# The expert stage of a streaming-encoder layer: weight splits in pieces of 1024 columns instead of 512, products with the high part of a weight first

## The chip, the cores and the metric

The program runs on one core of one Trainium2 chip. Its time is the device time of one execution in microseconds (us); the kernel before was executed three times for it. One further execution was recorded by the hardware profiler, and all rows below are from that record. The engines are named as in the profile: PE multiplies matrices (PEld is its weight load), ACT and DVE are the scalar and the vector engine, POOL and SP issue transfers here, each in the order in which its instructions stand.

## The reference

One layer of an encoder over 1024 tokens of 1024 features in float32: a mixer (pooling branch and gated recurrent branch), then a mixture of experts, then a norm. The change lies in the mixture. Each token is routed to two of 32 experts, and each expert computes, for its tokens:

```python
xt = rmsnorm(x, g_ffn).reshape(T, D)               # T = 1024, D = 1024
# top-1 group of 4, then the top-2 experts of its 8 -> expert_id, gate
hid = silu(xb @ w_gate[e]) * (xb @ w_up[e])        # (128, 1024) @ (1024, 512), twice
yb  = hid @ w_down[e]                              # (128, 512) @ (512, 1024)
y   = zeros((T, D)).at[tok].add(yb * gate)         # weighted sum of a token's two experts
```

Each expert has 6 MiB of float32 weights: 2 MiB each of gate, up and down.

## The kernel before

The program has two parts. The mixer and the router run first, on two halves of 512 tokens; their instructions are the same before and after the change. The expert stage follows, from about 713 us to 1303 us of the span, and a final norm ends the program.

**The stage.** A block of 128 token slots is computed for every expert (a dynamic loop ahead of the stage would take further blocks, L1245; it ran no iteration in this record). For expert e, PE's order is written out by hand (L1341 to 1365): `gate_up(e, 0)`, in whose middle `htrans(e - 1)` transposes the hidden values of the expert before; `gate_up(e, 1)`; `xtrans(e + 1)`, which transposes the next expert's tokens; and `down(e - 1)`. The order on ACT and DVE is made by a scheduler when the program is built. SP's and POOL's order around the stage is that of the code.

**Products in three parts.** PE gets a float32 matrix as a high part, rounded to the format fp32r, and a low part that holds the rest. `split` (L224) makes them: ACT copies the source into the high part (L225), DVE subtracts the high part from the source (L226). `mm3` (L243) multiplies high by high (L244), high by low (L245) and low by high (L246), 512 columns each, into one PSUM tile. One expert has 48 such products for gate and up (tiles `gu`) and 24 for down (tiles `y`), 72 in all.

**Pieces.** `piece` (L1172) splits one 512-column quarter of a weight slot: tiles `whi` (high) and `wlo` (low) of 512 columns, four buffers each. An expert takes 24 pieces. A piece's buffers are free once its three products are done. The tokens are split in `xtrans` (L1161), four transposes and one split of 512 columns at a time, in two PSUM tiles of tag `tr`; the hidden values in `htrans` (L1201), a third user of `tr`. `down` (L1213) has two PSUM tiles of 512 columns (tag `yo`), which ACT copies out by two instructions (L1224) before POOL scatters the rows to `yd` (L1228).

**Weight slots.** Weights come in transfers of 1 MiB, six for an expert, in the order in which they are used. `RING` (L932) lists 18 slots: 17 in memory that the mixer leaves, the last, `rawm`, in the stage's own. SP issues the transfer for the slot 18 further on when the slot's last piece has been split (L1177). Slots 0 to 16 are filled while the mixer ends, slot 17 (`load(17)`, L1237) just ahead of the stage.

**Entry and end.** Four pieces are split ahead of the first product, two before the dynamic loop (L1242) and two behind it (L1329). The first expert has no `down` in front of it, so expert 1's tokens are needed right after their transposes. At the end, `htrans(31)` and `down(31)` follow `down(30)` directly.

Of the kernel before, what the change touches and what calls it, by code (L numbers as in the profile page):

```python
# [10 lines left out]
F32 = mybir.dt.float32  # L11
F32R = mybir.dt.float32r
# [3 lines left out]
AF = mybir.ActivationFunctionType  # L16
# [24 lines left out]
def kernel(  # L41
# [4 lines left out]
    nc = tc.nc  # L46
# [17 lines left out]
    identf = cp.tile([P, P], F32, name="identf")  # L64
# [15 lines left out]
    rp = ctx.enter_context(tc.tile_pool(name="rp", bufs=2, side="right"))  # L80
    b8 = ctx.enter_context(tc.tile_pool(name="b8", bufs=4, side="right"))
# [161 lines left out]
    def mm3(o, ah, al, bh, bl, first, last):  # L243
        nc.tensor.matmul(o, ah, bh, start=first, stop=False)  # L244
        nc.tensor.matmul(o, ah, bl, start=False, stop=False)  # L245
        nc.tensor.matmul(o, al, bh, start=False, stop=last)  # L246
# [682 lines left out]
        eng.tensor_tensor(gates[:, hg, 0:1], q[0], q[1], op=OP.add)  # L929
        eng.tensor_tensor(gates[:, hg, 1:2], q[2], gates[:, hg, 0:1], op=OP.subtract)  # L930

    RING = (("t4", 2, 0), ("b2", 1, 0), ("r0", 3, 1), ("b2", 1, 0), ("r1", 6, 1), ("b8", 4, 2), ("rawm", 1, 3))  # L932
    ring = [(tag, pool) for tag, n, pool in RING for _ in range(n)]
    RA = len(ring)
    raws = {}
# [7 lines left out]

    def rawslot(n, shape, name):
        tag, pool = ring[n % RA]
        pool = rp if pool == 0 else b8 if pool == 2 else mp if pool == 3 else r0 if tag == "r0" else r1
        return pool.tile(shape, F32, name=name, tag=tag, bufs=2 if pool is rp else dict((a, b) for a, b, _ in RING)[tag])

    def load(n, q=nc.sync):
# [184 lines left out]
    for tag, shape, dt, bufs in (("xy", [D], F32, 4), ("xl", [2, FE], F32, 1), ("xh", [KT, P], F32, 1), ("hp", [2, 2, P], F32, 1),  # L1134
                                 ("hh", [4, P], F32, 1), ("hl", [4, P], F32, 1), ("whi", [FE], F32R, 4),
                                 ("rawm", [4, FE], F32, 1), ("wlo", [FE], F32R, 4)):
        ts = [mp.tile([P] + shape, dt, name=f"{tag}_{n}", tag=tag, bufs=bufs) for n in range(bufs)]
        if tag == "xy":
            xy = ts
        elif tag == "rawm":  # L1140
            raws[17] = ts[0]
        elif tag in ("wlo", "whi"):
            early[tag] = ts
        else:
            ov[tag] = ts[0]
# [15 lines left out]
    def xtrans(e):  # L1161
        xg = xgs[e]
        xh = mt([P, KT, P], F32R, f"xh{e}", "xh", 1)
        xl = mt([P, KT, P], F32R, f"xl{e}", "xl", 1)
        for k2 in range(2):
            tp = mq.tile([P, 4, P], F32, name=f"tp{e}{k2}", tag="tr", bufs=2)
            for k in range(4):
                nc.tensor.transpose(tp[:, k, :], xg[:, (4 * k2 + k) * P:(4 * k2 + k + 1) * P], identf)  # L1168
            split(xh[:, 4 * k2:4 * k2 + 4, :], xl[:, 4 * k2:4 * k2 + 4, :], tp)
        st["x", e] = (xh, xl)  # L1170

    def piece(ec, k, ld=True):  # L1172
        if (ec, k) in pre:
            return pre.pop((ec, k))
        n = where[ec]
        if ld and k == 0 and n + RA < 6 * NE:
            load(n + RA)  # L1177
        hi = mt([P, FE], F32R, f"wh{n}{k}", "whi", 4)
        lo = mt([P, FE], F32R, f"wl{n}{k}", "wlo", 4)
        split(hi, lo, raws[n][:, k, :])  # L1180
        return hi, lo

    def gate_up(e, n, mid=None):
        xh, xl = st["x", e]
        o = mq.tile([P, FE], F32, name=f"gu{e}{n}", tag="gu", bufs=4)
        for c in range(2):
            for k in range(4):
                wh, wl = piece((e, 2 * n + c), k)
                kk = 4 * c + k
                mm3(o, xh[:, kk, :], xl[:, kk, :], wh, wl, kk == 0, kk == KT - 1)  # L1190
                if mid and kk == 3:
                    mid[0](*mid[1:])
# [7 lines left out]

    def htrans(e):  # L1201
        hp = st["hp", e]
        tp = mq.tile([P, 4, P], F32, name=f"th{e}", tag="tr", bufs=2)
        for k in range(4):
            nc.tensor.transpose(tp[:, k, :], hp[:, k // 2, k % 2, :], identf)
        hh = mt([P, 4, P], F32R, f"hh{e}", "hh", 1)
        hl = mt([P, 4, P], F32R, f"hl{e}", "hl", 1)
        split(hh, hl, tp)
        st["h", e] = (hh, hl)
# [2 lines left out]

    def down(e):  # L1213
        hh, hl = st["h", e]
        yo = [mq.tile([P, 512], F32, name=f"y{e}{n}", tag="yo", bufs=2) for n in range(2)]
        for c in range(2):
            for k in range(2):
                kk = 2 * c + k
                for n in range(2):
                    wh, wl = piece((e, 4 + c), 2 * k + n)  # L1220
                    mm3(yo[n], hh[:, kk, :], hl[:, kk, :], wh, wl, kk == 0, kk == 3)
        ys = next_xy()
        for n in range(2):
            nc.scalar.activation(ys[:, n * 512:(n + 1) * 512], yo[n], AF.Copy)  # L1224
        return ys

    def scatter(e, ys):
# [17 lines left out]
    with tc.For_i(0, nov, 1) as it:  # L1245
# [15 lines left out]
        oidp = mq.tile([P, 2, 1], F32, name="oidp", tag="tr", bufs=2)  # L1261
# [11 lines left out]
        xg = xy[2]  # L1273
# [5 lines left out]
        for k2 in range(2):  # L1279
            tp = mq.tile([P, 4, P], F32, name="otp", tag="tr", bufs=2)  # L1280
            for k in range(4):
                nc.tensor.transpose(tp[:, k, :], xg[:, (4 * k2 + k) * P:(4 * k2 + k + 1) * P], identf)
            nc.vector.tensor_copy(xT[:, 4 * k2:4 * k2 + 4, :], tp)
# [19 lines left out]
        tp = mq.tile([P, 4, P], F32, name="otp", tag="tr", bufs=2)  # L1303
# [159 lines left out]
```

## Time and profile before

| | |
|---|---|
| time, median of 3 runs | 1349.5 us (1348.29 to 1351.13) |
| profiled execution, first to last instruction | 1349.2 us (the record gives no other time of it) |
| PE busy over the span | 1270.6 us, 94% |
| DVE busy over the span | 1023.3 us, 76% |
| ACT busy over the span | 828.6 us, 61% |
| last chain, share by engine | PE 88%, DVE 6%, DMA 3% |
| expert stage, 740 to 1290 us: PE / DVE / ACT busy | 549.9 / 519.2 / 519.8 of 550 us |
| granted PE clock in that stretch | 1.00 |

How to read it: the shares over the span mix a mixer, in which ACT and DVE have room, with a stage in which three engines are busy nearly all the time. Products on PE overlap, so the duration of one (about 0.39 us) says less than the distance from its start to the next one's start. "Idle" in a row is the time in which an engine had nothing to do ahead of the row's instruction, and the arrow names what ended it.

### The profile page before, as it was taken

How to read it: one execution, taken by the hardware profiler on the slowest of the kernel's cores; microseconds unless marked ns; L12 is line 12 of the kernel's file. 1: busy time of each engine (PE TensorE's matmuls, PEld its weight loads, DVE VectorE, ACT ScalarE, POOL GpSimd, SP SyncE). 2: the span in 40 equal slices, each digit the busy share in tenths (PEclk: the TensorE clock that was granted, in tenths of full speed). 3: DMA queues.
4: the chain of work that ended last, by engine and by line, in shares of the span. 5: the costliest groups of instructions: out<-in, count | busy, mean ns of one | idle time of the engine just before them, and what ended most of it. 6: DMA issues, size and time to landing. Idle time of an engine off the chain costs nothing.

```text
span 1349.2 us, 18579 instructions
## 1 busy us (share of the span) xinstructions
PE 1270.6 (94%) x6342; PEld 1050.6 (78%) x6342; DVE 1023.3 (76%) x1917; ACT 828.6 (61%) x1381; POOL 136.4 (10%) x209
## 2 busy tenths in 40 slices
PE   7999999999999999999968999999999999999960
PEld 6879888888988988888756777878777787877740
DVE  4586873456598687344287999999999999999977
ACT  5433422343533242233257999999999999999964
POOL 3110000000011000000042011011011101011004
PEclk9999999999999999999978999999999999999985
DMA  7332223344453222544767999999999999999255
GB/s 221 77 101 79 63 76 89 105 158 154 133 194 94 79 63 79 187 125 147 305 220 265 352 379 373 374 372 364 367 369 367 383 376 374 384 377 378 84 192 230
DMA packets 130698, 307.16 MB, mean 228 GB/s; under 512 B 15229, under 2 KB 89513, under 8 KB 106026
## 3 DMA queue, kind: packets, MB, share of 16 engines
q1 hardware_dynamic: 120378, 281.82, 59.0%
q0 software_dynamic: 9216, 16.80, 3.4%
q10 hardware_dynamic: 1008, 7.34, 1.4%
q8 instruction: 50, 0.82, 0.2%
q14 instruction: 46, 0.38, 0.1%
HBM read 295.43 MB, written 27.26 MB: 239 GB/s over the span
## 4 chain that ended last, share of the span: by engine, by line
PE 88%; DVE 6%; DMA 3%; ACT 1%; issue 1%; POOL 0%; SPq 0%; ACTq 0%; DVEq 0%; POOLq 0%
PE gu L245 9%; PE gu L246 9%; PE gu L244 8%; PE y L245 5%; PE y L246 4%; PE y L244 4%; PE ga L244 2%; PE ga L246 2%; PE ga L245 2%; PE gb L245 2%; PE gb L244 2%; PE gb L246 2%; PE vo L244 2%; PE tp L1168 2%; PE vo L245 2%; PE vo L246 2%
## 5 line engine op out<-in xcount | busy, mean ns | idle before, releaser
L226 DVE TENSOR_TENSOR wl<-rw,wh 128x512 fp32r<-128x512 f32 x760 | 477.0, 685 | 34.7 <-ACT wh L225 34.6
L225 ACT ACTIVATE wh<-rw 128x512 fp32r<-128x512 f32 x760 | 463.0, 631 | 32.6 <-PE y L246 11.9
L245 PE MATMUL gu<-wl,xh 128*128 128x512 f32 x508 | 201.6, 397 | 0.2 <-DVE wl L226 0.2
L244 PE MATMUL gu<-wh,xh 128*128 128x512 f32 x508 | 201.0, 396 | 0.8 <-ACT wh L225 0.4
L246 PE MATMUL gu<-wh,xl 128*128 128x512 f32 x508 | 198.7, 391 | 0.0
L245 PEld LDWEIGHTS gu<-wl,xh 128*128 128x128 f32 x508 | 95.4, 188 | 32.3 <-DVE wl L226 12.8
L244 PEld LDWEIGHTS gu<-wh,xh 128*128 128x128 f32 x508 | 95.4, 188 | 20.4 <-ACT wh L225 0.9
L246 PEld LDWEIGHTS gu<-wh,xl 128*128 128x128 f32 x508 | 95.4, 188 | 18.2 <-DVE xl L226 0.5
L244 PE MATMUL y<-wh,hh 128*128 128x512 f32 x256 | 102.7, 401 | 1.1 <-ACT hh L225 1.1
L245 PE MATMUL y<-wl,hh 128*128 128x512 f32 x256 | 103.5, 404 | 0.1
L246 PE MATMUL y<-wh,hl 128*128 128x512 f32 x256 | 100.6, 393 | 0.0
L245 PEld LDWEIGHTS y<-wl,hh 128*128 128x128 f32 x256 | 48.1, 188 | 21.6 <-DVE wl L226 12.4
L1157 POOL DMA_INDIRECT xy<-xtd,src x32 | 32.8, 1024 | 295.2 <-PE tp L1168 294.1
L244 PEld LDWEIGHTS y<-wh,hh 128*128 128x128 f32 x256 | 48.1, 188 | 10.7 <-ACT hh L225 1.3
L1228 POOL DMA_INDIRECT yd<-xy,dst x32 | 32.2, 1005 | 230.1 <-ACT xy L1224 230.1
L246 PEld LDWEIGHTS y<-wh,hl 128*128 128x128 f32 x256 | 48.1, 188 | 9.0 <-DVE hl L226 0.4
L226 DVE TENSOR_TENSOR xl<-tp,xh 128x512 fp32r<-128x512 f32 x64 | 41.1, 681 | 6.6 <-ACT xh L225 6.6
L1168 PE MATMUL tp<-identf,xy 128*128 128x128 f32 x256 | 34.0, 277 | 9.1 <-issue 9.1
L1168 PEld LDWEIGHTS tp<-identf,xy 128*128 128x128 f32 x256 | 30.5, 143 | 13.3 <-issue 9.2
L1224 ACT ACTIVATE xy<-y 128x512 f32<-128x512 f32 x64 | 38.1, 595 | 3.1 <-PE y L246 1.4
L419 DVE SCALAR_TENSOR_TENSOR cv<-zt,chn,cv 128x512 f32<-128x512 f32 x48 | 36.0, 750 | 1.5
L225 ACT ACTIVATE xh<-tp 128x512 fp32r<-128x512 f32 x64 | 34.3, 584 | 0.4 <-PE tp L1168 0.4
(1238 smaller groups left out, 2803.0 us busy)
## 6 DMA issues: line engine op xcount, KB each, us to landing
rw<-in_w_e_down_dram SPq DMA_DIRECT2D x62, 1024.0 KB, 7.4
rw<-in_w_e_gate_dram SPq DMA_DIRECT2D x61, 1024.0 KB, 7.8
rw<-in_w_e_up_dram SPq DMA_DIRECT2D x61, 1024.0 KB, 7.4
x<-in_x_dram SPq DMA_DIRECT2D x12, 512.0 KB, 6.2
xtd<-xq SPq DMA_DIRECT2D x8, 512.0 KB, 2.9
z<-yd SPq DMA_DIRECT2D x4, 1024.0 KB, 12.0
yh<-yd SPq DMA_DIRECT2D x4, 1024.0 KB, 4.9
out_dram<-yh SPq DMA_DIRECT2D x8, 512.0 KB, 2.6
```

The source lines that it names most:

```text
L225: nc.scalar.activation(hi, src, AF.Copy)
L226: eng.tensor_tensor(lo, src, hi.bitcast(F32), op=OP.subtract)
L244: nc.tensor.matmul(o, ah, bh, start=first, stop=False)
L245: nc.tensor.matmul(o, ah, bl, start=False, stop=False)
L246: nc.tensor.matmul(o, al, bh, start=False, stop=last)
L419: nc.vector.scalar_tensor_tensor(cv, zt[:, j:j + HS], wj(j), cv, op0=OP.mult, op1=OP.add)
L1157: nc.gpsimd.indirect_dma_start(out=xgs[e], out_offset=None, in_=xtd, in_offset=bass.IndirectOffsetOnAxis(ap=src[:, e:e + 1], axis=0), boun ...
L1168: nc.tensor.transpose(tp[:, k, :], xg[:, (4 * k2 + k) * P:(4 * k2 + k + 1) * P], identf)
L1224: nc.scalar.activation(ys[:, n * 512:(n + 1) * 512], yo[n], AF.Copy)
L1228: sc = nc.gpsimd.indirect_dma_start(out=yd, out_offset=bass.IndirectOffsetOnAxis(ap=dst[:, e:e + 1], axis=0), in_=ys, in_offset=None, boun ...
```

## The change

Only the expert stage and what feeds it are edited.

- A piece is half a weight slot, 1024 columns, with three buffers each for its high and low part. An expert takes 12 pieces, and `split` runs on 1024 columns.
- `mm6` takes the place of `mm3`: for one piece the four products with the weight's high part stand first, then the two with its low part. The 72 products of an expert stay.
- `xtrans` fills one PSUM tile of eight transposes and splits it once, at 1024 columns; the tags `tr` and `yo` have one buffer of two banks in place of two buffers of one bank. `down` copies its result out with one ACT instruction of 1024 columns.
- The ring has 17 slots: `rawm` and `load(17)` ahead of the stage are gone, and its memory goes to the larger pieces. Slot 17 is loaded behind the dynamic loop.
- Ahead of the first product two pieces of 1024 are split before the loop, the third after it.

```diff
-    RING = (..., ("b8", 4, 2), ("rawm", 1, 3))
+    RING = (..., ("b8", 4, 2))
...
-        for k2 in range(2):
-            tp = mq.tile([P, 4, P], F32, name=f"tp{e}{k2}", tag="tr", bufs=2)
-            for k in range(4):
-                nc.tensor.transpose(tp[:, k, :], xg[:, (4 * k2 + k) * P:(4 * k2 + k + 1) * P], identf)
-            split(xh[:, 4 * k2:4 * k2 + 4, :], xl[:, 4 * k2:4 * k2 + 4, :], tp)
+        tp = mq.tile([P, KT, P], F32, name=f"tp{e}", tag="tr", bufs=1)
+        for k in range(KT):
+            nc.tensor.transpose(tp[:, k, :], xg[:, k * P:(k + 1) * P], identf)
+        split(xh, xl, tp)
...
-        hi = mt([P, FE], F32R, f"wh{n}{k}", "whi", 4)
-        lo = mt([P, FE], F32R, f"wl{n}{k}", "wlo", 4)
-        split(hi, lo, raws[n][:, k, :])
+        hi = mt([P, 2, FE], F32R, f"wh{n}{j}", "whi", 3)
+        lo = mt([P, 2, FE], F32R, f"wl{n}{j}", "wlo", 3)
+        split(hi, lo, raws[n][:, 2 * j:2 * j + 2, :])
...
+    def mm6(os, ah, al, piece, first, last):
+        wh, wl = piece
+        for i in range(2):
+            nc.tensor.matmul(os[i], ah[i], wh[:, i, :], start=first[i], stop=False)
+            nc.tensor.matmul(os[i], al[i], wh[:, i, :], start=False, stop=False)
+        for i in range(2):
+            nc.tensor.matmul(os[i], ah[i], wl[:, i, :], start=False, stop=last[i])
...
-        yo = [mq.tile([P, 512], F32, name=f"y{e}{n}", tag="yo", bufs=2) for n in range(2)]
+        yo = mq.tile([P, 2, FE], F32, name=f"y{e}", tag="yo", bufs=1)
...
-        for n in range(2):
-            nc.scalar.activation(ys[:, n * 512:(n + 1) * 512], yo[n], AF.Copy)
+        nc.scalar.activation(ys, yo.rearrange("p n f -> p (n f)"), AF.Copy)
...
-    load(17)
...
-    for n in range(2, 4):
-        pre[((0, 0), n)] = piece((0, 0), n, False)
```

PE, start of `down(18)`, before. The names: `tp20` are expert 20's transposes, `y180` and `y181` the two halves of expert 18's result, `wh116k` and `wl116k` the high and low part of quarter k of weight slot 116, `hh18` and `hl18` those of the hidden values.

```order
L1168 MATMUL tp200_10754<-identf_63,xy_2_6256 128x128 x4
L1168 MATMUL tp201_10761<-identf_63,xy_2_6256 128x128 x4
L244 MATMUL y180_10768<-wh1160_10772,hh18_10651 128x512
L245 MATMUL y180_10768<-wl1160_10773,hh18_10651 128x512
L246 MATMUL y180_10768<-wh1160_10772,hl18_10652 128x512
L244 MATMUL y181_10769<-wh1161_10779,hh18_10651 128x512
L245 MATMUL y181_10769<-wl1161_10780,hh18_10651 128x512
L246 MATMUL y181_10769<-wh1161_10779,hl18_10652 128x512
```

The same place on PE now; `wh1160` and `wl1160` are half a slot:

```order
L1165 MATMUL tp20_9725<-identf_63,xy_2_6256 128x128 x8
L1183 MATMUL y18_9736<-wh1160_9739,hh18_9646 128x512
L1184 MATMUL y18_9736<-wh1160_9739,hl18_9647 128x512
L1183 MATMUL y18_9736<-wh1160_9739,hh18_9646 128x512
L1184 MATMUL y18_9736<-wh1160_9739,hl18_9647 128x512
L1186 MATMUL y18_9736<-wl1160_9740,hh18_9646 128x512 x2
```

A low part was needed by the second product of a piece of three; it is now needed by the fifth of six.

DVE, around the hand-over from expert 20's gate and up products to `down(19)` (weight slots 122 and 123), before; `hp20` is the product of silu(gate) and up, `xl21` the low part of expert 21's tokens:

```order
L226 TENSOR_TENSOR wl1222_11007<-rw122_10330,wh1222_11006 128x512
L1198 TENSOR_TENSOR hp20_10966<-hp20_10966,gu201_10905 128x512
L226 TENSOR_TENSOR xl21_10973<-tp210_10974,xh21_10972 128x512
L226 TENSOR_TENSOR xl21_10973<-tp211_10981,xh21_10972 128x512
L226 TENSOR_TENSOR wl1223_11014<-rw122_10330,wh1223_11013 128x512
L226 TENSOR_TENSOR wl1230_11023<-rw123_10360,wh1230_11022 128x512
```

The same place on DVE now:

```order
L226 TENSOR_TENSOR wl1220_9907<-rw122_9425,wh1220_9906 128x1024
L226 TENSOR_TENSOR wl1221_9917<-rw122_9425,wh1221_9916 128x1024
L1203 TENSOR_TENSOR hp20_9884<-hp20_9884,gu201_9839 128x512
L226 TENSOR_TENSOR wl1230_9929<-rw123_9452,wh1230_9928 128x1024
L226 TENSOR_TENSOR xl21_9891<-tp21_9892,xh21_9890 128x1024
L226 TENSOR_TENSOR wl1231_9939<-rw123_9452,wh1231_9938 128x1024
```

Three quarters of slot 122 stood ahead of the token split; now the whole of slot 122 and half of slot 123 stand ahead of it.

ACT, from the first expert's tokens (`xh0`) to the second's (`xh1`), now; before, the two were pairs of 512 columns with wh10 to wh43, sixteen pieces of 512, between them:

```order
L225 ACTIVATE xh0_6502<-tp0_6504 128x1024
L225 ACTIVATE wh11_6538<-rw1_5242 128x1024
L225 ACTIVATE wh20_6551<-rw2_5519 128x1024
L225 ACTIVATE wh21_6561<-rw2_5519 128x1024
L225 ACTIVATE wh30_6573<-rw3_5295 128x1024
L1202 ACT_TABLE_LOAD
L1202 ACTIVATE hp0_6593<-gu00_6515 128x512
L225 ACTIVATE wh31_6583<-rw3_5295 128x1024
L225 ACTIVATE wh40_6615<-rw4_5354 128x1024
L225 ACTIVATE wh41_6625<-rw4_5354 128x1024
L225 ACTIVATE wh50_6646<-rw5_5407 128x1024
L225 ACTIVATE xh1_6599<-tp1_6601 128x1024
```

Between the two token splits stand eight pieces of 1024, of which the last, wh50, is half of a weight slot that stood wholly behind `xh1` before.

## Rows read from the trace of the kernel before

**Rows 1.** Page, its head: span and instructions.

```profile
span 1349.2 us, 18579 instructions
```

**Rows 2.** Stretches: busy us per engine (instructions), granted clock, DMA share, GB/s.

```profile
700.00:720.00 20.00, 8.02 (x61) 6.78 (x61) 11.74 (x37) 8.26 (x16) 10.85 (x19) 0.59 0.63 213
740.00:1290.00 550.00, 549.94 (x2529) 438.50 (x2528) 519.22 (x844) 519.75 (x904) 57.67 (x57) 1.00 0.92 351
```

**Rows 3.** Chain that ended last, in order of time: start us, us, what.

```profile
906.03 0.87 PE tp L1168 x8
924.32 0.87 PE tp L1168 x8
...
1302.89 0.61 ACT xy L1224
```

**Rows 4.** Waits of PE's weight load, 740 to 1290 us: total, times, longest.

```profile
PEld y L245 <- DVE wl L226: 12.4, 30, 0.4
PEld gu L245 <- DVE wl L226: 12.3, 30, 0.4
```

**Rows 5.** Timeline of PE in down: start us, us, instruction.

```profile
908.79 0.39 PE L244 MATMUL y<-wh,hh 128*128 128x512 f32 x1
909.19 0.50 PE L245 MATMUL y<-wl,hh 128*128 128x512 f32 x1
909.52 0.40 PE L246 MATMUL y<-wh,hl 128*128 128x512 f32 x1
```

**Rows 6.** Timeline of PE in gate and up, with htrans between.

```profile
914.58 0.39 PE L244 MATMUL gu<-wh,xh 128*128 128x512 f32 x1
914.95 0.50 PE L245 MATMUL gu<-wl,xh 128*128 128x512 f32 x1
915.29 0.40 PE L246 MATMUL gu<-wh,xl 128*128 128x512 f32 x1
...
916.20 0.39 PE L245 MATMUL gu<-wl,xh 128*128 128x512 f32 x1
...
919.62 0.39 PE L245 MATMUL gu<-wl,xh 128*128 128x512 f32 x1
```

**Rows 7.** Groups of the stage, 740 to 1290 us: count, busy, mean ns, idle.

```profile
L226 DVE TENSOR_TENSOR wl<-rw,wh 128x512 fp32r<-128x512 f32 x720 | 450.8, 685 | 30.8 <-ACT wh L225 30.8
L225 ACT ACTIVATE xh<-tp 128x512 fp32r<-128x512 f32 x60 | 32.0, 584 | 0.0
L1198 DVE TENSOR_TENSOR hp<-hp,gu 128x512 f32<-128x512 f32 x30 | 20.4, 679 | 0.0
```

**Rows 8.** Groups of the mixer at 1024 columns: the same two split lines.

```profile
L225 ACT ACTIVATE wb04h<-wb04r 128x1024 fp32r<-128x1024 f32 x1 | 1.1, 1065 | 1.1 <-PE yb L245 1.1
...
L226 DVE TENSOR_TENSOR wv0001l<-raw,wv0001h 128x1024 fp32r<-128x1024 f32 x1 | 2.7, 2729 | 0.0
L226 DVE TENSOR_TENSOR wu03l<-wu03r,wu03h 128x1024 fp32r<-128x1024 f32 x1 | 1.2, 1227 | 1.1 <-ACT wu03h L225 1.1
```

**Rows 9.** Timeline of the stage's entry, ACT and PE.

```profile
715.59 0.60 ACT L225 ACTIVATE xh<-tp 128x512 fp32r<-128x512 f32 x1 [0.26 <-PE tp L1168]
...
715.98 0.63 PE L245 MATMUL gu<-wlo,xh 128*128 128x512 f32 x1
...
716.40 0.46 PE L246 MATMUL gu<-whi,xl 128*128 128x512 f32 x1
...
722.35 1.28 ACT L1197 ACT_TABLE_LOAD   x1
...
732.52 0.39 PE L246 MATMUL gu<-wh,xl 128*128 128x512 f32 x1
```

**Rows 10.** Timeline of PE between down(30) and down(31).

```profile
1294.94 0.39 PE L246 MATMUL y<-wh,hl 128*128 128x512 f32 x1
...
1297.55 0.50 PE L246 MATMUL y<-wh,hl 128*128 128x512 f32 x1
```

**Rows 11.** Waits of SP's queue, 740 to 1290 us: total, times, longest.

```profile
SPq L959 <- DVE wl L226: 440.8, 167, 4.0
```

More of the change, by code (lines that the diff above doesn't have):

```diff
@@ L930, in rt_gate @@
         eng.tensor_tensor(gates[:, hg, 1:2], q[2], gates[:, hg, 0:1], op=OP.subtract)
-    RING = (("t4", 2, 0), ("b2", 1, 0), ("r0", 3, 1), ("b2", 1, 0), ("r1", 6, 1), ("b8", 4, 2), ("rawm", 1, 3))
+    RING = (("t4", 2, 0), ("b2", 1, 0), ("r0", 3, 1), ("b2", 1, 0), ("r1", 6, 1), ("b8", 4, 2))
     ring = [(tag, pool) for tag, n, pool in RING for _ in range(n)]
@@ L945, in rawslot @@
         tag, pool = ring[n % RA]
-        pool = rp if pool == 0 else b8 if pool == 2 else mp if pool == 3 else r0 if tag == "r0" else r1
+        pool = rp if pool == 0 else b8 if pool == 2 else r0 if tag == "r0" else r1
         return pool.tile(shape, F32, name=name, tag=tag, bufs=2 if pool is rp else dict((a, b) for a, b, _ in RING)[tag])
@@ L1134 @@
     for tag, shape, dt, bufs in (("xy", [D], F32, 4), ("xl", [2, FE], F32, 1), ("xh", [KT, P], F32, 1), ("hp", [2, 2, P], F32, 1),
-                                 ("hh", [4, P], F32, 1), ("hl", [4, P], F32, 1), ("whi", [FE], F32R, 4),
-                                 ("rawm", [4, FE], F32, 1), ("wlo", [FE], F32R, 4)):
+                                 ("hh", [4, P], F32, 1), ("hl", [4, P], F32, 1), ("whi", [2, FE], F32R, 3),
+                                 ("wlo", [2, FE], F32R, 3)):
         ts = [mp.tile([P] + shape, dt, name=f"{tag}_{n}", tag=tag, bufs=bufs) for n in range(bufs)]
@@ L1139 @@
             xy = ts
-        elif tag == "rawm":
-            raws[17] = ts[0]
         elif tag in ("wlo", "whi"):
@@ L1164, in xtrans, with piece @@
         xl = mt([P, KT, P], F32R, f"xl{e}", "xl", 1)
-        for k2 in range(2):
-            tp = mq.tile([P, 4, P], F32, name=f"tp{e}{k2}", tag="tr", bufs=2)
-            for k in range(4):
-                nc.tensor.transpose(tp[:, k, :], xg[:, (4 * k2 + k) * P:(4 * k2 + k + 1) * P], identf)
-            split(xh[:, 4 * k2:4 * k2 + 4, :], xl[:, 4 * k2:4 * k2 + 4, :], tp)
+        tp = mq.tile([P, KT, P], F32, name=f"tp{e}", tag="tr", bufs=1)
+        for k in range(KT):
+            nc.tensor.transpose(tp[:, k, :], xg[:, k * P:(k + 1) * P], identf)
+        split(xh, xl, tp)
         st["x", e] = (xh, xl)
-    def piece(ec, k, ld=True):
-        if (ec, k) in pre:
-            return pre.pop((ec, k))
+    def piece(ec, j, ld=True):
+        if (ec, j) in pre:
+            return pre.pop((ec, j))
         n = where[ec]
-        if ld and k == 0 and n + RA < 6 * NE:
+        if ld and j == 0 and n + RA < 6 * NE:
             load(n + RA)
-        hi = mt([P, FE], F32R, f"wh{n}{k}", "whi", 4)
-        lo = mt([P, FE], F32R, f"wl{n}{k}", "wlo", 4)
-        split(hi, lo, raws[n][:, k, :])
+        hi = mt([P, 2, FE], F32R, f"wh{n}{j}", "whi", 3)
+        lo = mt([P, 2, FE], F32R, f"wl{n}{j}", "wlo", 3)
+        split(hi, lo, raws[n][:, 2 * j:2 * j + 2, :])
         return hi, lo
+    def mm6(os, ah, al, piece, first, last):
[5 more added lines that the diff above has]
+            nc.tensor.matmul(os[i], ah[i], wl[:, i, :], start=False, stop=last[i])
     def gate_up(e, n, mid=None):
@@ L1186, in gate_up @@
         for c in range(2):
[L1187 to L1192, printed above, removed]
+            for j in range(2):
+                kk = 4 * c + 2 * j
+                mm6([o, o], [xh[:, kk + i, :] for i in range(2)], [xl[:, kk + i, :] for i in range(2)],
+                    piece((e, 2 * n + c), j), (kk == 0, False), (False, kk == KT - 2))
+            if mid and c == 0:
+                mid[0](*mid[1:])
         return o
@@ L1202, in htrans @@
         hp = st["hp", e]
-        tp = mq.tile([P, 4, P], F32, name=f"th{e}", tag="tr", bufs=2)
+        tp = mq.tile([P, KT, P], F32, name=f"th{e}", tag="tr", bufs=1)[:, 0:4, :]
         for k in range(4):
@@ L1218, in down @@
                 kk = 2 * c + k
-                for n in range(2):
-                    wh, wl = piece((e, 4 + c), 2 * k + n)
-                    mm3(yo[n], hh[:, kk, :], hl[:, kk, :], wh, wl, kk == 0, kk == 3)
+                mm6([yo[:, n, :] for n in range(2)], [hh[:, kk, :]] * 2, [hl[:, kk, :]] * 2,
+                    piece((e, 4 + c), k), (kk == 0, kk == 0), (kk == 3, kk == 3))
         ys = next_xy()
-        for n in range(2):
-            nc.scalar.activation(ys[:, n * 512:(n + 1) * 512], yo[n], AF.Copy)
+        nc.scalar.activation(ys, yo.rearrange("p n f -> p (n f)"), AF.Copy)
         return ys
@@ L1260 @@
         nc.vector.tensor_scalar(rk, ranks, ebs[:, 1:2], None, op0=OP.subtract)
-        oidp = mq.tile([P, 2, 1], F32, name="oidp", tag="tr", bufs=2)
+        oidp = mq.tile([P, KT, P], F32, name="oidp", tag="tr", bufs=1)[:, 0, 0:2].rearrange("p (a e) -> p a e", e=1)
         for n in range(2 * TT):
@@ L1278 @@
         xT = ov["xh"]
[L1279 to L1283, printed above, removed]
+        tp = mq.tile([P, KT, P], F32, name="otp", tag="tr", bufs=1)
+        for k in range(KT):
+            nc.tensor.transpose(tp[:, k, :], xg[:, k * P:(k + 1) * P], identf)
+        nc.vector.tensor_copy(xT, tp)
         er = nc.sync.value_load(oe_i[0:1, 0:1], min_val=0, max_val=NE - 1)
@@ L1302 @@
         nc.vector.tensor_tensor(hp, hp, ps[1].rearrange("p (c q k) -> p c k q", c=2, k=2), op=OP.mult)
-        tp = mq.tile([P, 4, P], F32, name="otp", tag="tr", bufs=2)
+        tp = mq.tile([P, KT, P], F32, name="otp", tag="tr", bufs=1)[:, 0:4, :]
         for k in range(4):
@@ L1307 @@
         nc.vector.tensor_copy(hT, tp)
-        yo = [mq.tile([P, 512], F32, name=f"oy{n}", tag="yo", bufs=2) for n in range(2)]
+        yo = mq.tile([P, 2, FE], F32, name="oy", tag="yo", bufs=1)
+        yo = [yo[:, n, :] for n in range(2)]
         for c in range(2):
```

## The prediction

> **What bounds the kernel now.** I read the head of the page, then the chain that ended last, then what PE waited for, and at last the timeline around those waits. The span is 1349.2 us [rows 1]; the sum below is made against it, and it stands 0.3 us under the median of the three runs. From 740 to 1290 us PE is busy for 549.9 of 550 us, at a granted clock of 1.00, with DVE and ACT at 94% [rows 2]. Busy is not at its peak, though. In the chain one expert's transposes start at 906.03, the next one's at 924.32 [rows 3]: an expert takes 18.29 us. Where nothing is waited for, products start 0.228 us apart: from 916.20 to 919.62 there are 15 steps [rows 6]. What the page calls busy hides two short stalls per expert, 30 of each kind in this stretch, all of the product with a low part, waiting for DVE's subtraction [rows 4].
>
> The price of a stall is read from starts, not from the 0.4 us of idle, part of which is normal. In `down` the steps are 908.79 to 909.19 and on to 909.52, 0.73 us where two plain steps take 0.456 [rows 5]: 0.27 lost. In gate and up they are 914.58 to 914.95 and 915.29, 0.71 us [rows 6]: 0.25 lost. The first comes where DVE has just done two jobs for the tokens and the hidden values beside its weight pieces, the second after ACT has copied out `y`. The lead in split pieces, four of three products each or 4 x 0.684 = 2.7 us, is too short for them.
>
> **The change part by part.**
>
> *The two stalls.* Three pieces of six products are a lead of 3 x 1.37 = 4.1 us, and a low part is wanted four products (0.9 us) after its high part, not one. I go through the worst place, the hand-over to `down`, with the order shown, taking zero where PE has done the high products of the last up piece (1211). PE: two low products and the transposes (0.87 [rows 3]) end at 1.3; six products per piece put the start of 1231 at 5.4 and its low products at 6.3. ACT: wh1230 from 0.2 with 1.07 at 1024 columns [rows 8]; xh21 from 1.4 to 2.5 (PSUM to SBUF took 0.584 at 512 [rows 7], so I take 1.07 here too; 2 x 0.584 = 1.17 is the upper bound); wh1231 until 3.6, wanted at 5.4. DVE: hp20 from 0.8, 0.68 [rows 7]; wl1230, xl21 and wl1231 at 1.23 each [rows 8], done at 5.2, wanted at 6.3. So 1.1 us remain on DVE and 1.8 on ACT, and I expect no stall here. At the second place ACT's copy of `y` stands behind wh1190, whose buffer comes free only 0.45 us before `down` ends; the copy then begins at 0.75 us after `down`, wh1191 is done at 2.8 and is wanted at 4.5. Both stalls go: 30 x (0.27 + 0.25) = 15.6 us, bounded by 0 and 15.6.
>
> *The split itself.* 685 ns twice against 1227 once on DVE [rows 7, 8] is 0.14 us less per pair. That is not on PE's path: it counts only in that it keeps the lead.
>
> *Order of the products.* The 72 products and their weight loads stay. Whether the spacing of 0.228 moves when high products come first, or when `down` changes between two banks, no row shows. 512 columns at 2.4 GHz are 0.213 us, so the lower bound is 72 x 30 x 0.015 = 32 us of gain. The products with a wait that was met and those without one stand equally far apart in rows 6, so I take 0, and keep 3 us to either side for the range.
>
> *Entry of the stage.* Here the larger pieces cost. Before, the first product started when four transposes had been split. Now `xh0` starts at 715.59, where the second half did [rows 9], and ends at 716.7; `xl0` ends at 717.9, and the second product wants it. PE then runs through the eight pieces of expert 0 until 728.6 and the transposes of expert 1 until 729.5. ACT is late here: wh30 ends at 724.0 (its buffer was held until 722.9), the table load takes 1.28 [rows 9] and hp0 0.58, then come wh31, wh40, wh41, wh50 and `xh1`, until 731.2. DVE has wl40, hp0, wl41 and `xl1`, until 732.4. So at 732.5 PE starts the second product of expert 1; before, it started the twelfth at 732.52 [rows 9]. Ten products, 2.3 us lost. Bounds: 0, if ACT's jobs overlap more than this, and 3.5, as follows: in this stretch the granted clock is 0.59 [rows 2], and while it was low two products stood 0.42 apart, 715.98 to 716.40 [rows 9]; if the pause up to 717.9 holds six more products at that spacing, 6 x 0.19 = 1.2 us come on top.
>
> *End of the stage.* `htrans(31)` follows `down(30)` directly. Before, the last product of `down(30)` started at 1294.94 and the third of `down(31)`, which waited for the low part of the hidden values, at 1297.55 [rows 10]: 2.6 us. Now ACT has wh1910, the 1024-column copy and hh31 in a row, about 1.0 + 1.0 + 0.6 from the last product on, and hl31 adds 0.7: the second product starts at 3.4. That is 0.8 and one product later: 1.0 us. After the last product of all, ACT's copy took 0.61 [rows 3] and takes 1.07: 0.5 us. Bounds for both together 0.5 and 2.
>
> *Ring of 17.* SP's queue waited 440.8 us in 167 waits for DVE to free a slot [rows 11]: slots are late, transfers are not. Seventeen slots are 17/6 of an expert, 50 us of work. Six MiB in 17.8 us in place of 18.3 asks 3% more of a queue that moves 351 GB/s at a share of 0.92 [rows 2]. Could it move no more, it would fall back 0.52 us per expert, 16 us in all, less than the 50 that the slots hold. Cost 0. `load(17)` behind the loop leaves the first gather of tokens less company; I take 0 for it and up to 0.8 us of gain.
>
> *One PSUM buffer in place of two.* The next writer of `tr` after the token transposes is `htrans`, 36 products or 8.2 us later by PE's order; by the steps above `xl21` has been read by 3.9 us. `yo` is next written an expert later. Cost 0. The Trainium skill ("Perfetto Trace Analysis", section Matmuls) advises the opposite of this edit: independent matmul groups should rotate through PSUM banks, so that evacuating one overlaps the next group's products. Taken at its word, PE would stand through both splits after each set of transposes; that result is a rival below. No row before the change shows PE waiting for a PSUM tile.
>
> Sum: -15.6 + 2.3 + 1.0 + 0.5 = -11.8, so 1337.4 against the span and 1337.7 against the median; I say 1337.5. Its own range is 1332 to 1343: the entry and end bounds (-3 to +2), and 3 us either way for the spacing.
>
> **The rivals.**
>
> *DVE becomes the bound (slower).* An expert needs 13 DVE operations of 1024 columns and two of 0.68 us: 13 x 1.227 + 1.36 = 17.3 us, against PE's 18.29 - 0.52 = 17.77. That is 97%. From 1.262 us per operation on DVE decides, and from 1.302 on the kernel is slower than before. For it: one of the mixer's took 2.729 [rows 8]. Against it: that is a single one; and DVE's operations overlap when queued, since 720 of 685 ns were 450.8 us of busy time, 626 ns each [rows 7], so 17.3 overstates. At 1.35 us it would be 18.9 per expert: 30 x 0.62 + 3.8 = 22 slower, 1372 us.
>
> *The PSUM tile is waited for (slower).* PE idle through xh and xl at each expert, 1.07 + 1.23 = 2.3 us, 69 in all less the 11.8: 1406 us. This is the result of the skill's rule above; the 8.2 us between the two writers speak against it.
>
> *Half of it stays.* Six products wait together for one ACT instruction, and a handover that I take as 0.1 us is longer; one of the two stalls remains: 1349.2 - 7.8 + 3.8 = 1345.
>
> *Transfers take the place of the splits (no change).* The queue can't give 3% more and the slots were never full; the period stays at 18.29, and entry and end cost: 1349 to 1353. For it: a DMA share of 0.92, although the stretch holds the end of the stage, when no weights are left to load. Against it: SP waits for slots.
>
> **How the numbers follow.** A measurement of this kernel tells 0.2%, 2.7 us, from no change. The forecast has 0.67, half of it 0.11; both are faster: 0.78. Transfers, or stalls that move to another place in full: 0.12, counted as the same. DVE-bound 0.08 and the PSUM wait 0.02 are slower: 0.10. The range has to leave out no more than 2 in 10: from 1330, where the spacing helps and the entry costs nothing, to 1347, with the half case and its entry bound.
>
> **What would show it.** Right: the waits of rows 4 gone, 17.8 us between one expert's transposes and the next; DVE at 1.23 and ACT at 1.07 per piece; the second product at 717.9 and a stall of 2 to 3 us before expert 1's products; SP still waiting for DVE. Wrong: PE waiting once per expert at a first high product (ACT late) or at `htrans` (the PSUM tile), DVE without idle time, ACT or DVE waiting for a weight transfer, or a spacing other than 0.228 in the stage.

## The result and the profile after

Before ran in 1349.0 us (median of 4), the changed kernel in 1339.7 (median of 4, 1336.7 to 1340.6): a ratio of 0.992, 95% interval 0.991 to 0.993. The profiled execution after has a span of 1337.8 us, 11.4 less than [rows 1]. One execution of e4 took 1863.2 us and one of e6 3276.3 us; both are left out of the times and ratios below.

The head of the page, and the same two stretches as in [rows 2] (busy us and instructions of PE, PEld, DVE, ACT, POOL; granted clock; DMA share; GB/s):

```profile
span 1337.8 us, 17537 instructions
```

```profile
700.00:720.00 20.00, 9.59 (x60) 7.45 (x60) 9.72 (x24) 8.01 (x11) 9.78 (x16) 0.54 0.51 169
740.00:1290.00 550.00, 548.12 (x2585) 454.69 (x2584) 509.18 (x462) 466.87 (x491) 85.71 (x58) 1.00 0.92 355
```

ACT has lost 53 us of work against [rows 2], DVE 10. The chain shows two neighbouring experts, to be set beside [rows 3]:

```profile
903.40 0.87 PE tp L1165 x8
...
921.14 0.87 PE tp L1165 x8
```

They are 17.74 us apart, where there were 18.29. The waits from 740 to 1290 us (total, times, longest) say why. Both lines of [rows 4] are gone; what PE still waits for comes once, at the end. Now ACT waits for PE to give buffers back:

```profile
ACT wh L225 <- PE gu L1184: 31.1, 123, 0.3
ACT wh L225 <- PE y L1184: 30.1, 94, 1.8
DVE wl L226 <- ACT wh L225: 27.4, 62, 2.1
...
PE y L1183 <- ACT hh L225: 1.7, 1, 1.7
...
PE y L1184 <- DVE hl L226: 0.2, 1, 0.2
```

The groups of the split, for their mean beside [rows 7] (count, busy, mean ns, idle before; here over the whole span):

```profile
L226 DVE TENSOR_TENSOR wl<-rw,wh 128x1024 fp32r<-128x1024 f32 x381 | 459.8, 1222 | 46.8 <-ACT wh L225 36.1
L225 ACT ACTIVATE wh<-rw 128x1024 fp32r<-128x1024 f32 x381 | 400.3, 1059 | 80.2 <-PE gu L1184 40.2
```

And SP's queue, as in [rows 11]: it still waits for slots, not for transfers.

```profile
SPq L959 <- DVE wl L226: 428.2, 168, 3.6
```

The loss is at the stage's two ends. PE at the entry, beside [rows 9]:

```profile
710.44 1.97 PE L1165 MATMUL tp<-identf,xy 128*128 128x128 f32 x8 [7.93 <-issue]
713.52 0.79 PE L1183 MATMUL gu<-whi,xh 128*128 128x512 f32 x1 [1.11 <-ACT xh L225]
714.78 0.79 PE L1184 MATMUL gu<-whi,xl 128*128 128x512 f32 x1 [0.47 <-DVE xl L226]
715.37 0.63 PE L1183 MATMUL gu<-whi,xh 128*128 128x512 f32 x1
715.80 0.63 PE L1184 MATMUL gu<-whi,xl 128*128 128x512 f32 x1
...
727.36 1.04 PE L1165 MATMUL tp<-identf,xy 128*128 128x128 f32 x8
729.51 0.49 PE L1183 MATMUL gu<-wh,xh 128*128 128x512 f32 x1 [1.11 <-ACT xh L225]
730.79 0.50 PE L1184 MATMUL gu<-wh,xl 128*128 128x512 f32 x1 [0.79 <-DVE xl L226]
...
732.11 0.63 PE L1183 MATMUL gu<-wh,xh 128*128 128x512 f32 x1
732.54 0.63 PE L1184 MATMUL gu<-wh,xl 128*128 128x512 f32 x1
```

Products stand 0.43 us apart until 718.4 (before, until 716.4 [rows 9]), and again from 732.1 to 734.7, where 0.228 is the pace of the stage: after a pause PE's clock was at its lower level (1.2 GHz) once more. At the end, beside [rows 10], the same:

```profile
1281.08 0.60 PE L1210 MATMUL th<-identf,hp 128*128 128x128 f32 x4
1283.33 0.49 PE L1183 MATMUL y<-wh,hh 128*128 128x512 f32 x1 [1.65 <-ACT hh L225]
1284.06 0.50 PE L1184 MATMUL y<-wh,hl 128*128 128x512 f32 x1 [0.23 <-DVE hl L226]
...
1285.63 0.63 PE L1183 MATMUL y<-wh,hh 128*128 128x512 f32 x1
1286.06 0.63 PE L1184 MATMUL y<-wh,hl 128*128 128x512 f32 x1
```

```profile
731.00:735.00 4.00, 4.00 (x13) 3.03 (x13) 2.09 (x2) 2.00 (x2) 0.00 (x0) 0.62 0.84 322
1285.00:1288.50 3.50, 3.50 (x10) 2.72 (x9) 1.23 (x1) 1.06 (x1) 0.00 (x0) 0.52 0.40 77
```

The last two lines are two stretches of the same kernel, with granted clocks of 0.62 and 0.52.

To compare all kernels (e1 stands for e1_six_small, and so on), each profile's span is cut at the transposes of the tokens (rows "tp" in PE's timeline) and at the end of the last copy of `y` on ACT. The tail behind it is 45 to 47 us everywhere.

| kernel | first tp at | to expert 2's tp | next 29 experts (each) | expert 31's tp to last copy | ratio to before (95%) |
|---|---|---|---|---|---|
| before | 713.58 | 27.82 | 530.03 (18.28) | 32.06 | 1 |
| after | 710.44 | 33.20 | 514.27 (17.73) | 34.33 | 0.992 (0.991-0.993) |
| e1 | 713.42 | 28.38 | 514.27 (17.73) | 31.51 | 0.986 (0.985-0.988) |
| e2 | 713.25 | 29.40 | 530.04 (18.28) | 32.02 | 1.000 (0.999-1.001) |
| e3 | 714.21 | 35.00 | 523.94 (18.07) | 32.50 | 0.999 (0.998-1.000) |
| e4 | 717.47 | 29.02 | 514.26 (17.73) | 32.74 | 0.995 (0.993-0.996) |
| e5 | 713.40 | 27.84 | 514.27 (17.73) | 32.24 | 0.988 (0.987-0.990) |
| e6 | 711.92 | 35.44 | 528.82 (18.24) | 33.53 | 1.005 (1.004-1.007) |
| e7 | 708.62 | 29.95 | 514.23 (17.73) | 32.72 | 0.991 (0.989-0.992) |
| e8 | 711.25 | 27.19 | 514.26 (17.73) | 30.54 | 0.988 (0.986-0.989) |
| e9 | 708.17 | 31.16 | 514.27 (17.73) | 32.71 | 0.992 (0.991-0.993) |
| e10 | 712.01 | 29.76 | 514.27 (17.73) | 31.28 | 0.989 (0.988-0.991) |
| e11 | 711.16 | 27.90 | 514.26 (17.73) | 31.48 | 0.987 (0.986-0.989) |
| e12 | 713.18 | 28.06 | 514.26 (17.73) | 32.72 | 0.988 (0.986-0.990) |

Profile to profile the change comes to -3.1 + 5.4 - 15.8 + 2.3 - 0.2 (tail) = -11.4 us.

### The profile page after: what moved, and what is told of

Same layout as the page of the kernel before. It is cut to its first block, busy times and chain, and to the rows that moved or that the text cites. A ratio compares the mean times of both kernels' runs of the same rounds, so it can differ in the third digit from the quotient of the medians.

```text
span 1337.8 us, 17537 instructions
## 1 busy us (share of the span) xinstructions
PE 1256.3 (94%) x6342; PEld 1056.4 (79%) x6342; DVE 1000.4 (75%) x1501; ACT 762.3 (57%) x933; POOL 164.5 (12%) x209
## 4 chain that ended last, share of the span: by engine, by line
PE 87%; DVE 6%; DMA 3%; ACT 2%; issue 1%; POOL 0%; SPq 0%; ACTq 0%; DVEq 0%; POOLq 0%
PE gu L1184 9%; PE gu L1183 9%; PE gu L1186 9%; PE y L1184 4%; PE y L1183 4%; PE y L1186 4%; PE ga L244 2%; PE ga L246 2%; PE ga L245 2%; PE gb L244 2%; PE gb L245 2%; PE gb L246 2%; PE vo L244 2%; PE tp L1165 2%; PE vo L245 2%; PE vo L246 2%
## 5 line engine op out<-in xcount | busy, mean ns | idle before, releaser
L226 DVE TENSOR_TENSOR wl<-rw,wh 128x1024 fp32r<-128x1024 f32 x381 | 459.8, 1222 | 46.8 <-ACT wh L225 36.1
L225 ACT ACTIVATE wh<-rw 128x1024 fp32r<-128x1024 f32 x381 | 400.3, 1059 | 80.2 <-PE gu L1184 40.2
L1186 PE MATMUL gu<-wl,xh 128*128 128x512 f32 x506 | 157.0, 392 | 0.0
L1155 POOL DMA_INDIRECT xy<-xtd,src x32 | 60.6, 1893 | 274.1 <-PE tp L1165 273.0
L1186 PE MATMUL y<-wl,hh 128*128 128x512 f32 x256 | 80.0, 394 | 0.0
L226 DVE TENSOR_TENSOR xl<-tp,xh 128x1024 fp32r<-128x1024 f32 x32 | 39.0, 1218 | 1.9 <-ACT xh L225 1.9
L225 ACT ACTIVATE xh<-tp 128x1024 fp32r<-128x1024 f32 x32 | 32.9, 1028 | 9.3 <-PE tp L1165 9.2
L1227 ACT ACTIVATE xy<-y 128x1024 f32<-128x1024 f32 x32 | 32.3, 1009 | 5.1 <-PE y L1186 5.1
```

The source lines that it names most:

```text
L1155: nc.gpsimd.indirect_dma_start(out=xgs[e], out_offset=None, in_=xtd, in_offset=bass.IndirectOffsetOnAxis(ap=src[:, e:e + 1], axis=0), boun ...
L1186: nc.tensor.matmul(os[i], ah[i], wl[:, i, :], start=False, stop=last[i])
L1227: nc.scalar.activation(ys, yo.rearrange("p n f -> p (n f)"), AF.Copy)
```

## The experiments

The theory was that of the prediction: the gain is the longer lead of split pieces over PE, the loss the coarser hand-over at both ends. Against it stood the fewer, longer split instructions, the order of the products, the ring, and for the loss the clock.

**e1_six_small.** The lead without the large pieces.

```
- "whi", [FE], F32R, 4    "wlo", [FE], F32R, 4    RING ... ("rawm", 1, 3)
+ "whi", [FE], F32R, 6    "wlo", [FE], F32R, 6    RING ... ("b8", 4, 2)
```

> The kernel before with pieces of 512 columns, its old order of products and its old entry and end, but 17 slots and six buffers each for high and low parts instead of four (the same memory as three of 1024). Theory (the lead in split pieces is what counts): the waits of PE for DVE's low parts go, an expert takes 17.75 us, entry and end stay as before (27.98 us from the first transposes to those of expert 2), so 1349 - 15.6 = 1333 to 1334, ratio to before 0.988 to 0.989. Rival A (fewer, longer split instructions are what counts): DVE stays at 2 x 0.685 per pair, the waits stay, 18.2 us per expert, ratio 0.997 to 1.000. Rival B (the order of the products counts, low parts wanted later): the waits stay in part, since a low part is wanted one product after its high part: ratio 0.994 or more.

1330.6 us, ratio 0.986. From 740 to 1270 us only this wait is left between PE, ACT and DVE:

```profile
DVE wl L226 <- ACT wh L225: 13.8, 59, 0.3
```

The two stalls go with pieces of 512 columns in the old order, DVE being busy for 515.8 of 530 us. So neither long instructions nor the new order are needed. Entry and end cost next to nothing (+0.6 and -0.6 us in this profile). This kernel is faster than both before and after.

**e2_ring_only.** The ring of e1 with four buffers.

```
- load(17)      RING ... ("b8", 4, 2), ("rawm", 1, 3))
+               RING ... ("b8", 4, 2))
```

> The kernel before with the ring of 17 slots alone (its eighteenth slot and load(17) gone), four buffers of 512 columns. Theory: an expert stays at 18.29 us, the two waits per expert for DVE stay, and only the first gather may land up to 1.2 us earlier (5.2 instead of 6.4 us): ratio 0.999 to 1.000. Rival (the ring or the earlier start of the stage brings the gain): 0.992 to 0.998, the stage beginning 3 us earlier.

1349.1 us, ratio 1.000; the period is that of before. The ring and `load(17)` do nothing, as the theory had it. One thing did differ in this profile, though the products of the entry are those of before: nine steps behind the first transposes are 0.43 us long, where before has one (715.98 to 716.40 [rows 9]), and the entry takes 29.40 us in place of 27.82. The last of them:

```profile
713.25 1.97 PE L1166 MATMUL tp<-identf,xy 128*128 128x128 f32 x8 [9.01 <-issue]
...
719.05 0.63 PE L244 MATMUL gu<-whi,xh 128*128 128x512 f32 x1
719.48 0.45 PE L245 MATMUL gu<-wlo,xh 128*128 128x512 f32 x1
```

What the low level behind the first transposes costs thus differs by 1.6 us between these two executions. The removal of `load(17)` does not explain it: e1, e8 and e11, which lack it too and have the same products there, show eight, two and six such steps.

**e3_old_order.** The changed kernel with the products of each half as they were.

```
+ for i in range(2):
+     mm3(os[i], ah[i], al[i], wh[:, i, :], wl[:, i, :], first[i], last[i])
```

> The changed kernel with the old order of products in each half of a piece (high part, low part of the weight, low part of the tokens), so that a low part is wanted one product after its high part. Theory: the order costs nothing, since three pieces are a lead of 4.1 us and DVE still has 0.4 us in hand at the hand-over: 17.73 us per expert, ratio to before 0.991 to 0.994 as the changed kernel. Rival (the order is needed): PE waits for DVE once per expert, 0.1 to 0.3 us each, 3 to 8 us more: 0.995 to 0.998.

1347.8 us, ratio 0.999: the theory fell, and the rival too was short of this. An expert takes 18.07 us, 9.7 us more than in the changed kernel over the 29 experts of the table, and DVE's waits are back, at a shorter length each:

```profile
PEld y L245 <- DVE wl L226: 7.0, 29, 0.2
PEld gu L245 <- DVE wl L226: 6.5, 29, 0.2
```

The theory had counted only when a low part is wanted (0.68 us earlier in the old order). It had left out when a high buffer is given back: behind the sixth product of a piece instead of the fourth, 0.46 us later. ACT's timeline in e3 shows what this does:

```profile
896.27 1.06 ACT L225 ACTIVATE wh<-rw 128x1024 fp32r<-128x1024 f32 x1 [0.30 <-PE y L246]
...
899.00 1.06 ACT L225 ACTIVATE wh<-rw 128x1024 fp32r<-128x1024 f32 x1 [0.30 <-PE y L246]
900.48 1.03 ACT L1224 ACTIVATE xy<-y 128x1024 f32<-128x1024 f32 x1 [0.41 <-PE y L246]
901.40 2.94 ACT L225 ACTIVATE wh<-rw 128x1024 fp32r<-128x1024 f32 x3
```

Between `xh` and the copy of `y` ACT splits three pieces here, four in the changed kernel, whose last is this one:

```profile
909.35 1.06 ACT L225 ACTIVATE wh<-rw 128x1024 fp32r<-128x1024 f32 x1 [0.29 <-PE y L1184]
910.32 1.01 ACT L1227 ACTIVATE xy<-y 128x1024 f32<-128x1024 f32 x1
```

So in e3 the third piece of the gate weights has to wait until `y` is complete and copied, and PE waits for its low part, at 903.77:

```profile
903.36 0.48 PE L244 MATMUL gu<-wh,xh 128*128 128x512 f32 x1
903.77 0.50 PE L245 MATMUL gu<-wl,xh 128*128 128x512 f32 x1
904.10 0.39 PE L246 MATMUL gu<-wh,xl 128*128 128x512 f32 x1
```

The wait in `down` is the hand-over. The split at 896.27, of the last down piece, has to wait for its buffer too; DVE has the low part done at about 898.95, and PE waits for it until 899.03:

```profile
898.80 0.39 PE L244 MATMUL y<-wh,hh 128*128 128x512 f32 x1
899.03 0.48 PE L245 MATMUL y<-wl,hh 128*128 128x512 f32 x1
```

No run takes the two effects of the order apart, the later want of the low part and the earlier release of the high one.

**e5_order_only.** The order alone, on the kernel before.

```
+ ps = [piece((e, 2 * n + c), 2 * j + i) for i in range(2)]
+ for i in range(2):    # ah, al against the high part of ps[i]
+ for i in range(2):    # ah against the low part of ps[i]
```

> The kernel before with nothing changed but the order of products: over each pair of 512-column pieces the four products of the high parts first, then the two of the low parts; four buffers each, ring of 18, old entry and end. Theory after the run with the old order (a low part wanted 0.68 us later is worth what a longer lead is worth, as long as it is more than the 0.27 us that is missing): the two waits per expert go or nearly go, 17.75 to 17.9 us per expert, ratio to before 0.988 to 0.992. Rival (it is the lead in buffers that counts, the order helps only pieces of 1024): 18.2 us per expert, 0.996 to 1.000.

1332.9 us, ratio 0.988, 17.73 us per expert. With four buffers of 512 columns and the ring of 18, PE waits for nobody from 740 to 1270 us; ACT waits for PE:

```profile
ACT wh L225 <- PE gu L1186: 17.9, 89, 0.2
ACT wh L225 <- PE y L1186: 17.6, 90, 0.2
```

The rival falls. What was missing, 0.27 us, is less than the 0.68 us by which the order puts off the want of the low part.

**e6_two_large.** The changed kernel, two buffers of 1024 columns.

```
- "whi", [2, FE], F32R, 3    "wlo", [2, FE], F32R, 3
+ "whi", [2, FE], F32R, 2    "wlo", [2, FE], F32R, 2
```

> The changed kernel with two buffers of 1024 columns instead of three, so that the lead is four halves as before. Theory: a piece's split can start only when the piece two before it has been used, and the token and hidden splits (1.2 + 0.7 + 0.7 us of DVE per expert) have no lead to hide in: 0.5 to 2.6 us per expert lost, ratio to before 1.004 to 1.05. Rival (long pieces and the order are enough without the third buffer): 17.73 us per expert, 0.992.

1355.9 us, ratio 1.005; 18.24 us per expert, the entry 2.2 us dearer than after, the end 0.8 cheaper. The theory holds at its lower end: with the lead of before, even the new order leaves two stalls.

```profile
PEld y L1186 <- DVE wl L226: 13.0, 29, 0.5
...
PEld gu L1186 <- DVE wl L226: 7.1, 31, 0.3
```

**e4_busy_pauses** and **e7_busy_pauses_2.** Products that nothing reads fill PE's pauses.

```
+ for _ in range(n):    # 22 or 0 before tp0, 8 or 3 behind it, 9 behind tp1, 8 behind th31
+     nc.tensor.matmul(o, w[:, 0:P], w[:, 0:FE], start=True, stop=True)
```

> The changed kernel with 47 products added that nothing reads, in PE's pauses: 22 while the first tokens are gathered, 8 behind the first transposes, 9 behind those of expert 1, 8 behind those of the last hidden values. Theory (beyond the hand-over time, entry and end cost by the low level of PE's clock after a pause): the products that stood 0.42 to 0.43 apart stand 0.228 apart; the first transposes take 1.04 in place of 1.97 us, nine products of expert 0 and six of expert 1 and of the last one save 0.2 us each, 5 us at most, of which the later splits may take back two: ratio to before 0.988 to 0.991. Rival (the splits set entry and end whatever the clock is): the products are closer but wait for ACT and DVE as long again, ratio 0.992 or more. Second rival: the added products do not hold the clock, the spacing stays at 0.43 and the time is as long as the changed kernel's or longer.

1341.5 us, ratio 0.995: longer than the changed kernel. The 22 products did not start while the tokens were gathered, but at 709.48, and held the first transposes up to 717.47. Behind that the clock is at 1.00, and from there to expert 2 it takes 29.02 us instead of 33.20, the end 32.74 instead of 34.33.

> As e4_busy_pauses, without the 22 products ahead of the first transposes (which ran from 709.48 to 717.47 and held them up) and with 3 instead of 8 behind these. Theory: the pauses of expert 1 and of the end keep the high clock (1.5 and 1.6 us less than in the changed kernel), the first one begins at the low clock and saves 0 to 1 us: ratio to before 0.989 to 0.990. Rival (only the 22 products held the clock, through the entry): the products of expert 1 stand 0.43 apart again, and only the end is better: 0.991 to 0.9925.

1335.5 us, ratio 0.991, its interval overlapping that of the change. Entry 29.95 us, end 32.72, and none of the products that count stands 0.43 behind another. The profile agrees with the theory; the ratio lies just outside its range and inside the rival's, and e12 takes part of its proof away.

**e9_token_halves** and **e12_halves_two_tiles.** The changed kernel with the tokens of experts 0 and 1 split in halves; in e9 both halves lie in one PSUM tile, in e12 in two.

```
+ split(xh[:, 4 * k2:4 * k2 + 4, :], xl[:, 4 * k2:4 * k2 + 4, :], tps[k2])    # k2 = 0, 1, for e < 2; in e9 tp[:, 4 * k2:4 * k2 + 4, :]
```

> The changed kernel, with the tokens of experts 0 and 1 alone split in two halves of 512 columns again, each half as soon as its four transposes are done. Theory (the coarse token split is the hand-over part of the entry's cost): the second product of expert 0 starts 2.6 us after the first transposes instead of 4.3, the one of expert 1 about 2.2 instead of 3.4 us after its own; with the slow products that this saves, 2 to 4.5 us: ratio to before 0.9885 to 0.9905. Rival (ACT's and DVE's queues, not the size of the token split, set expert 1's start): only expert 0 gains, 1.0 to 1.7 us: 0.991 to 0.9915.

1337.3 us, ratio 0.992, as the change: the edit made a wait of its own. The second four transposes write the other half, a bank of its own, of the tile whose first half is being split, and wait until that is done:

```profile
724.52 0.60 PE L1166 MATMUL tp<-identf,xy 128*128 128x128 f32 x4
727.42 0.66 PE L1166 MATMUL tp<-identf,xy 128*128 128x128 f32 x4 [2.30 <-DVE xl L226]
```

> e9_token_halves with the second half of the transposes of experts 0 and 1 in a tile of its own (a bank of the one that the results use later), so that they need not wait until the first half has been split: in e9_token_halves they waited 1.41 and 2.30 us for that. Theory (the size of the token split is the hand-over part of the entry's cost): the second product of expert 0 starts 2.6 to 2.9 us after the first transposes, where the changed kernel took 4.34, and from the first transposes to those of expert 2 it takes 29 to 31 us in place of 33.2: ratio to before 0.989 to 0.991. Rival (the clock alone sets the entry, or ACT's queue sets expert 1's start): 32 to 33 us, 0.9915 to 0.9925.

1334.2 us, ratio 0.988. The entry takes 28.06 us, nearly what it took before: the rival falls. Some of that is luck: behind the first transposes one step is 0.43 us long here, as before, and eight are in e9, 0.2 us each. Expert 0's second product starts 2.5 us behind the first transposes instead of 4.3; expert 1's still waits for DVE until 729.95, 2.9 us behind its own. The end, whose instructions are those of the changed kernel, shows something else:

```profile
1278.67 0.60 PE L1218 MATMUL th<-identf,hp 128*128 128x128 f32 x4
1280.93 0.50 PE L1191 MATMUL y<-wh,hh 128*128 128x512 f32 x1 [1.66 <-ACT hh L225]
1281.65 0.50 PE L1192 MATMUL y<-wh,hl 128*128 128x512 f32 x1 [0.22 <-DVE hl L226]
...
1283.14 0.39 PE L1192 MATMUL y<-wh,hl 128*128 128x512 f32 x1
1283.37 0.39 PE L1191 MATMUL y<-wh,hh 128*128 128x512 f32 x1
```

The pauses are as long as after, yet the products stay 0.23 apart. So a pause of this length can bring the clock down but need not.

How much of the median after is clock can be bounded. The mean granted clock is on record for every execution: 0.969 to 0.971 in the four of after, 0.974 on average in 50 of before, 0.973 to 0.975 in e7's, 0.972 to 0.974 in e12's. One minus the clock, times the span, is about 40, 35, 35 and 36 us: an estimate of the clock that was withheld, some of it while PE had nothing to do. So on average the changed kernel's executions had 5 us more of it withheld than before, and those of e7 and e12 no more than before. What share of the 5 us fell on products in the stage is not shown.

**e8_end_inside.** e1 with the last hidden values split inside expert 30's down projection.

```
+ ys = down(e - 1, (htrans, e) if e == NE - 1 else None)    # called behind its second k
```

> e1_six_small with the last expert's hidden values transposed and split behind the second of the four groups of products of expert 30's down projection, instead of after all of them. Theory (at the end PE waits only for that split): from the transposes th31 at 1279.24 to the first product at 1280.90 and the third at 1281.62 some 1.4 us are lost in e1_six_small; they go, ratio to before 0.985. Rival (ACT and DVE have no room there): the waits move to the weight pieces of the last down projection, 0.986 to 0.987 as e1_six_small.

The end is 1.0 us shorter than in e1 (30.54 against 31.51); 1331.7 us against e1's 1330.6 (or e11's 1331.9) shows no gain. Inconclusive: it is smaller than what the starts scatter.

**e10_all_small** and **e11_six_again.** e8 with the order of e5, and e1 once more.

```
+ e8_end_inside with mm_pair(...) of e5_order_only in gate_up and down
```

> Everything that helped, together: pieces of 512 columns in six buffers, ring of 17, old entry, the last hidden values split inside expert 30's down projection, and the order of e5_order_only (high parts of a pair first). Theory: the stage runs at PE's own pace of 17.73 us per expert already with the order or the buffers alone, so both together add nothing there; only the 1.0 us of the end stays: ratio to before 0.985 to 0.9865, DVE with more idle time before each wait. Rival (order and buffers still add up): a period below 17.73 us and 0.983 or less.

> The kernel of e1_six_small once more, beside e10_all_small on one chip. Theory: again 0.985 to 0.988, and 0 to 2 us above e10_all_small. Rival (the stage's start, which lay between 702.2 and 706.5 us in the profiles so far, decides between kernels this close): the two differ by less than their scatter, in either direction.

e11 1331.9 us (0.987), e10 1334.6 (0.989): e10 misses its theory, and is the longer of the two. The period does not fall below 17.73: PE's pace. e10's entry is dearer than e11's (29.76 against 27.90), but the order is not shown to be the reason: e5, with the same order there, took 27.84. Ten steps behind e10's first transposes are 0.43 us long, six of e11's, one of e5's. The order does cost at the end, where both halves of `y` are complete only with the last two products and the next down projection waits for the copies:

```profile
1280.66 0.50 PE L1183 MATMUL y<-wh,hh 128*128 128x512 f32 x1 [0.81 <-ACT xy L1235]
```

## Why the prediction was right, and where it was not

*The two stalls* (-15.6): -15.8, with the waits of [rows 4] gone and 17.73 us per expert against 17.77 foretold. At the hand-over DVE's second low part of that stretch is done at 907.95 (started at 906.73, 1.22 long) and wanted at 909.15: 1.2 us in hand, where the sum had 1.1.

*The reason given for it* was half of it. The longer lead and the later want of the low part stood in one sum; e3, e5 and e6 take them apart. With large pieces both are needed: three buffers in the old order gain 0.21 us per expert (18.07), two buffers in the new order 0.04. With small pieces one is enough (e1, e5). The sum also missed that the order frees high buffers two products earlier, and so moves a split ahead of the copy of `y` on ACT (e3).

*The split itself* and *the spacing* (0): DVE takes 1.222 us, ACT 1.059, the spacing is 0.228. The price for DVE as the bound, 1.262, was not reached.

*Entry* (+2.3, bounds 0 to 3.5): +5.4 in the profile, outside its bounds. The hand-over was sized well: the second product was put 4.3 us behind the first transposes and came 4.34 behind them. Expert 1's second product came 20.35 us behind the first transposes; before, the twelfth, ten products on, came 18.94 behind them. With 2.3 us for the ten, 3.7 were lost up to there. Of these, 1.2 are six more products at the low level than before, just what the upper bound had added, and 2.5 the hand-over, put at 2.3.

The step that failed is the low clock behind expert 1's pause, at which the prediction had put nothing: six products stood 0.43 us apart there, the transposes of the hidden values took 0.95 us in place of 0.60, and the last 1.7 us of the loss are nearly all this. The 1.2 us behind the first pause may not be the change's: e2 had eight more such steps than before, and e11 five more, with the products of before.

With the pauses filled (e7) the entry costs 2.1 us, close to the hand-over alone. With two token splits in halves (e12) it costs 0.2, with one slow step behind the first transposes as before. So the coarse token split is at the root of the loss, by its pauses or by the clock that followed them, though e12's 0.2 owes something to a clock that rose early.

*End* (+1.5, bounds 0.5 to 2): +2.3, of which 1.6 are slow products, as e9 and e12 show with 32.7 for the same instructions; without them it is +0.7.

*Ring* and *PSUM* (0): e2 confirms the first. For the second, no wait of PE on a PSUM tile appears in the stage. The Trainium skill ("Perfetto Trace Analysis", section Matmuls), which asks for rotating banks, is not borne out by these rows of after; e10's 0.81 us, where two down projections follow each other in the same banks, is a place where it holds. e9's 2.30 us is another matter, a wait for a tile whose two halves lie in banks of their own.

*Not foreseen*: the stage began 3.1 us earlier. e1 and e2, without `load(17)` as well, begin at 713.4 and 713.3 as before, so that is not the change's. Without it the terms come to -8.3 us in this execution (the medians: -9.3), where the sum had -11.8: in the profile's own total, this hid the error at entry and end. That the span of 1337.8 us stands beside the sum's 1337.4 is luck to that extent.

## What to carry to other kernels

A stall of a few tenths of a microsecond per round can be cured by a longer lead, or by wanting the late operand later in each group: try the reorder alone first, it is free in memory. Larger pieces give back their lead in coarser release and hand-over; in equal memory and in the old order, six small buffers freed PE of its waits (17.73 us per expert) and three large ones did not (18.07). In the new order the period is the same; the changed kernel is behind e1 (0.992 against 0.986) at entry and end, and e12, with large weight pieces and small first token splits, is at 0.988. Price the first and last round of a pipeline apart from the steady one, with the clock that PE has there.

## What was not expected of the hardware

After the same pause (1.65 and 0.23 us, 1.66 and 0.22) the granted clock was 0.52 in one profiled execution and full in another, products 0.43 against 0.23 us apart. And with the same instructions ahead of it the first gather of tokens was issued anywhere from 701.3 (e7) to 706.5 us (e3): a difference of 2 us between two single profiles is no evidence. Among executions of one kernel the longer ones had the lower mean clock: e3 took 1345.1 us at 0.974 and 1352.5 at 0.969.
